# Plain float32 matmuls in place of three float32r products in a two-layer hybrid decoder (mLSTM, differential attention, routed experts)

## The chip, the cores and the metric

The kernel runs on one core of a Trainium2 chip. The metric is device time in microseconds (us) of one execution, the median over runs; lower is better. Engines are named as in the profile: PE is TensorE (matmuls), PEld its weight loads, DVE is VectorE, ACT is ScalarE, POOL is GpSimd, SP issues most of the DMAs.

## The reference

Two layers over 512 tokens of 1024 channels, all in float32. Each layer is a token mixer and then a mixture of experts; both read a normed input that is scaled and shifted by a modulation vector and both add their result, times a gate from the same vector, to the residual. Cut to what matters:

```python
D_MODEL, SEQ, DEPTH = 1024, 512, 2
A_HEADS, A_QK_DIM, A_V_DIM, A_CHUNK = 4, 128, 256, 128     # layer 0: mLSTM
B_HEADS, B_HEAD_DIM, B_V_DIM = 8, 64, 128                  # layer 1: differential attention
N_EXPERTS, N_GROUPS, TOP_K, D_EXPERT = 16, 4, 2, 512

def trunk(x, c, ...):
    for l in range(DEPTH):
        mod = silu(c) @ w_ada[l] + b_ada[l]                # 1024 x 6144: shift, scale, gate, twice
        sh1, sc1, g1, sh2, sc2, g2 = split(mod, 6)
        h = rms(x, norm1[l]) * (1 + sc1) + sh1
        x = x + g1 * (mlstm_mixer(h) if l % 2 == 0 else diff_attention(h))
        h = rms(x, norm2[l]) * (1 + sc2) + sh2
        x = x + g2 * grouped_moe(h, w_router, router_bias, w_gu[l], w_down[l])

def mlstm_mixer(h):
    proj = h @ w_in                                        # 1024 x 3080: q, k, v, o and 8 gate columns
    hout = mlstm_chunkwise(q, k, v, i_pre, log_f)          # 4 chunks of 128 tokens, a state between them
    return (rms(hout, h_norm) * sigmoid(o)) @ w_out        # 1024 x 1024

def diff_attention(h):
    q, k, v = split(h @ w_in)                              # 1024 x 3072
    a = softmax(q1 k1) - lam * softmax(q2 k2)              # per head, causal, q and k normed and rotated
    return rms(a @ v) @ w_out                              # 1024 x 1024

def grouped_moe(h):
    scores = sigmoid(h @ w_router)                         # one of 4 groups, the best 2 of its 4 experts
    for each expert e, tokens xb of e:
        gu = xb @ w_gu[e]                                  # 1024 x 1024
        yb = (silu(gu[:, :512]) * gu[:, 512:]) @ w_down[e] # 512 x 1024
    return sum over a token's two experts of gate_w * yb
```

## The kernel before

**Products.** Every large matrix product takes its weights from memory in float32 and makes two float32r parts of them: `split` (L205 to L210) copies the raw tile to `hi` on ACT (L208) and subtracts on DVE (L209; on POOL for the first strips) to get `lo`. The tokens are kept in two parts in the same way (`in_parts`, L343 and L344; `half_to_T`, L369 and L370). A product of 128 rows by 512 columns is then three matmuls that add up in one PSUM bank, high by high, high by low, low by high (`triple`, L212 to L217, for the experts and the output projections; L394 to L396 and L419 to L421 for the input projections):

```python
for ps, n, i in sorted(order, key=lambda o: o[1]) if last else order:
    w = (hi, lo, hi)[i][:, n * 512:(n + 1) * 512]
    T.matmul(ps, (xh, xh, xl)[i], w, start=first and i == 0, stop=last and i == 2)
```

In the names of the trace a trailing h or l is such a part: `guse64h` is the high part of row block 4 of expert 6's gate and up weights, `dnse50l` the low part of a block of expert 5's down weights. Transposes, attention scores, attention values, the mLSTM core and the routing are plain float32 matmuls already; so is the product of `diag` with the rows `yk` that come back from memory (L1278).

**Count of products.** The mLSTM's input projection has 192 products of 512 columns (q and k in `proj_cols`, v and o in `proj_rows`), the attention's 384 of 256 columns (12 strips `b00` to `bv6`), each output projection 64 of 512 columns (`out_proj`). An expert has 24 of 512 columns: 8 blocks of the inner dimension times `pg` and `pu`, then 4 blocks times `py0` and `py1`, on 128 gathered tokens; and 12 transposes of 128 columns (8 of its tokens, 4 of its activation). There are 16 experts in each layer.

**Order of the work.** The program is written out in order, with a small queue (`later`, `step`) that puts the latency-bound steps of the mixers (gates, chunks, heads, norms) between the steps of the projections; the framework's scheduler then orders the instructions of each engine, and each engine takes them in that order. One expert's pieces are put between those of the next: the transposes of the next tokens, the second half of gate and up, the first quarters of the next expert's, then the down product.

**Modulation.** `ada` (L225) loads four quarters of a 1024 x 1024 part of `w_ada`, scales each row block by an entry of silu(c) and adds them to `acc`: for layer 0 every other block in one step on DVE (L237), the rest as a scaling on ACT (L239) and an addition on POOL (L240). Six parts lie beside the mLSTM, four beside the attention.

**Weights ahead.** `load` issues the DMAs on SP into 4 buffers `raw` of 1 MB; for the experts `Prefetch` has 15 such places in all: 7 of its own, the 4 `raw` and the 4 in which the token parts lay.

**Results.** `keep` copies an expert's result from PSUM on ACT (L1332), multiplies it by the gate row on POOL (L1333) and scatters it to memory; the last expert's is added by matmuls (`results`, `add_to_tokens`), again in two parts.

Of the kernel before, what the change touches and what calls it, by code (L numbers as in the profile page):

```python
# [12 lines left out]
F32R = mybir.dt.float32r  # L13
# [8 lines left out]
P = 128  # L22
# [20 lines left out]
N_RAW = 4  # L43
N_RAW2 = 7
N_LO = 2
# [9 lines left out]
def trunk(ctx, tc, x, c, positions, norm1, norm2, w_ada, b_ada, a_w_in, a_b_if, a_h_norm, a_w_out,  # L55
# [7 lines left out]
    wsp = ctx.enter_context(tc.tile_pool(name="wsp", bufs=3))  # L63
# [15 lines left out]
    # Work of the tensor engine that waits for other engines is put between matmuls that don't.  # L79
# [35 lines left out]
    start = wsp.tile([P, 4, P], F32, tag="whi", name="start")  # L115
# [11 lines left out]
    def past(dst):  # L127
        """Column less row."""
# [43 lines left out]
    def hold(dst, kt=NK - 1):  # L172
        """Keeps a load from going ahead of those that the first matmuls wait for."""
# [31 lines left out]
    def split(raw, a, n, name, on=V):  # L205
        hi = wsp.tile([P, a, n], F32R, tag="whi", name=name + "h")
        lo = wsp.tile([P, a, n], F32R, tag="wlo", name=name + "l", bufs=N_LO)
        A.activation(hi, raw, AF.Copy)  # L208
        on.tensor_tensor(lo, raw, hi.bitcast(F32), op=ALU.subtract)  # L209
        return hi, lo  # L210

    def triple(p0, p1, xh, xl, hi, lo, first, last):  # L212
        hi, lo = hi.rearrange("p o n -> p (o n)"), lo.rearrange("p o n -> p (o n)")
        order = [(ps, n, i) for i in range(3) for n, ps in enumerate((p0, p1))]
        for ps, n, i in sorted(order, key=lambda o: o[1]) if last else order:
            w = (hi, lo, hi)[i][:, n * 512:(n + 1) * 512]
            T.matmul(ps, (xh, xh, xl)[i], w, start=first and i == 0, stop=last and i == 2)  # L217
# [7 lines left out]
    def ada(l, j):  # L225
        """Yields after each quarter of w_ada[l]'s columns of part j; their sums follow the last."""
# [1220 lines left out]
```

## Time and profile before

| | |
|---|---|
| median of 3 runs | 1370.02 us (1362.04, 1370.02, 1370.56) |
| profiled execution, first to last instruction | 1357.3 us |
| median less that span | 12.7 us |
| PE / PEld / DVE / ACT / POOL busy | 1210.1 / 956.6 / 1126.2 / 890.3 / 496.9 us |
| mean granted PE clock | 0.955 of full |

The profile gives the profiled execution's span; what lies around it is taken as the 12.7 us between it and the median. Matmuls overlap in the pipeline and a matmul's duration in the trace is longer than the time to the next one's start, so the rate of PE is read from the distance between starts. A plain float32 matmul leaves two records, a transpose or a float32r matmul one. The stages of the span are: start (0 to 34 us), the rest of layer 0's mixer with output projection and routing (to 316), its 16 experts (to 637), results and layer 1's projections with most heads (to 884), the last heads and the output projection (to 994), routing (to 1018), 16 experts (to 1338), the last results.

### The profile page before, as it was taken

How to read it: one execution, taken by the hardware profiler on the slowest of the kernel's cores; microseconds unless marked ns; L12 is line 12 of the kernel's file. 1: busy time of each engine (PE TensorE's matmuls, PEld its weight loads, DVE VectorE, ACT ScalarE, POOL GpSimd, SP SyncE). 2: the span in 40 equal slices, each digit the busy share in tenths (PEclk: the TensorE clock that was granted, in tenths of full speed). 3: DMA queues.
4: the chain of work that ended last, by engine and by line, in shares of the span. 5: the costliest groups of instructions: out<-in, count | busy, mean ns of one | idle time of the engine just before them, and what ended most of it. 6: DMA issues, size and time to landing. Idle time of an engine off the chain costs nothing. (4 is left out here: it accounts for less than half of the span.)

```text
span 1357.3 us, 18042 instructions
## 1 busy us (share of the span) xinstructions
PE 1210.1 (89%) x6082; PEld 956.6 (70%) x6082; DVE 1126.2 (83%) x1804; ACT 890.3 (66%) x1376; POOL 496.9 (37%) x305
## 2 busy tenths in 40 slices
PE   3899999887999999998899998878969999999996
PEld 3677777666777777775798878655747777777774
DVE  7956777877999999997867888867678999999996
ACT  5465666336777778775767676555537777877773
POOL 2644650821332332221552664524332233233211
PEclk7999999898999999999899999778979999999999
DMA  9777660757899999935351443304558999999904
GB/s 367 234 264 262 231 217 1 303 194 266 327 354 353 333 336 356 336 124 201 114 186 63 156 144 136 125 1 155 213 177 308 337 336 353 351 349 339 348 18 189
DMA packets 105586, 320.88 MB, mean 236 GB/s; under 512 B 14088, under 2 KB 26512, under 8 KB 104464
## 3 DMA queue, kind: packets, MB, share of 16 engines
q1 hardware_dynamic: 95120, 298.67, 60.3%
q0 software_dynamic: 10368, 20.99, 4.1%
q8 instruction: 50, 0.82, 0.2%
q14 instruction: 48, 0.39, 0.1%
HBM read 313.33 MB, written 23.07 MB: 248 GB/s over the span
## 5 line engine op out<-in xcount | busy, mean ns | idle before, releaser
L240 POOL TENSOR_TENSOR acc<-acc,ada 128x1024 f32<-128x1024 f32 x58 | 153.7, 2650 | 85.9 <-ACT ada L239 38.7
L1333 POOL TENSOR_TENSOR yoe<-yoe,grow 128x1024 f32<-128x1024 f32 x30 | 88.1, 2935 | 209.2 <-ACT yoe L1332 209.2
L1159 POOL DMA_INDIRECT xg<-h2d,lst x32 | 34.2, 1068 | 248.8 <-PE xTe L367 225.6
L239 ACT ACTIVATE ada<-ada,cact 128x1024 f32<-128x1024 f32 x58 | 64.7, 1144 | 31.4 <-DMA ada<-in_w_ada_dram 28.6
L864 ACT ACTIVATE p<-p,mx 128x128 f32<-128x128 f32 (+3 forms) x64 | 35.6, 557 | 38.2 <-DVE mx L863 38.2
L857 PE MATMUL s<-kTb,qTb 64*128 64x128 f32 (+3 forms) x128 | 45.9, 534 | 11.1 <-DVE mx L860 10.4
L307 POOL TENSOR_TENSOR qrs<-qrs,nhalf 128x4 f32<-128x4 f32 x32 | 36.0, 1131 | 51.0 <-DVE qrs L306 49.6
L1223 POOL DMA_INDIRECT yd<-yoe,lst x30 | 50.9, 1697 | 8.4 <-POOL yoe L1333 8.4
L367 PE MATMUL xTe<-ident,xg 128*128 128x128 f32 x256 | 39.0, 282 | 15.7 <-DMA xg<-h2d,lst 15.7
L452 POOL TENSOR_TENSOR wo<-wo,grow 128x1024 f32<-128x1024 f32 x16 | 40.1, 2528 | 29.6 <-DVE wos102l L209 14.9
L1194 ACT ACTIVATE acte<-pge 128x512 f32<-128x512 f32 (+1 forms) x34 | 19.2, 571 | 47.2 <-PE pge L217 47.2
L367 PEld LDWEIGHTS xTe<-ident,xg 128*128 128x128 f32 x256 | 32.1, 146 | 20.3 <-DMA xg<-h2d,lst 15.9
L860 DVE CUSTOM_DVE_ANT_0 p<-s,maskW 128x128 f32<-128x128 f32 (+3 forms) x64 | 29.9, 484 | 13.0 <-PE s L857 6.5
L307 POOL TENSOR_TENSOR ors<-ors,nhalf 128x2 f32<-128x2 f32 (+1 forms) x12 | 12.0, 1000 | 58.5 <-DVE ors L306 25.3
L237 DVE SCALAR_TENSOR_TENSOR acc<-ada,cact,acc 128x1024 f32<-128x1024 f32 x12 | 15.4, 1282 | 18.9 <-POOL acc L240 15.7
L857 PEld LDWEIGHTS s<-kTb,qTb 64*128 64x128 f32 x128 | 16.4, 200 | 19.6 <-DVE mx L860 12.0
L831 DVE TENSOR_TENSOR qrow<-qrow,qrs 128x256 f32<-128x256 f32 x32 | 24.3, 760 | 6.0 <-POOL qrs L307 5.9
L889 PE MATMUL o<-vb,aTs 128*128 128x128 f32 x160 | 26.7, 302 | 1.7 <-ACT aTs L881 0.9
L889 PEld LDWEIGHTS o<-vb,aTs 128*128 128x128 f32 x160 | 23.0, 210 | 6.7 <-ACT aTs L881 2.3
L369 ACT ACTIVATE xh0e<-xTe 128x512 fp32r<-128x512 f32 x32 | 19.0, 594 | 11.7 <-PE pue L217 7.1
L370 DVE TENSOR_TENSOR xl0e<-xTe,xh0e 128x512 fp32r<-128x512 f32 x32 | 21.9, 684 | 5.4 <-ACT xh0e L369 5.4
L251 PE MATMUL psada<-ident,acc 128*128 128x128 f32 x96 | 14.8, 287 | 13.0 <-DVE acc L276 12.4
(3698 smaller groups left out, 4866.1 us busy)
## 6 DMA issues: line engine op xcount, KB each, us to landing
we<-in_moe_w_gu_dram SPq DMA_DIRECT2D x128, 1024.0 KB, 6.8
we<-in_moe_w_down_dram SPq DMA_DIRECT2D x64, 1024.0 KB, 7.0
ada<-in_w_ada_dram SPq DMA_DIRECT2D x48, 1024.0 KB, 5.3
yk<-yd SPq DMA_DIRECT2D x8, 1024.0 KB, 6.9
wo<-in_a_w_out_dram SPq DMA_DIRECT2D x4, 1024.0 KB, 4.8
wo<-in_b_w_out_dram SPq DMA_DIRECT2D x4, 1024.0 KB, 4.7
x<-in_x_dram SPq DMA_DIRECT2D x4, 512.0 KB, 4.7
qk0w<-in_a_w_in_dram SPq DMA_DIRECT2D x2, 1024.0 KB, 13.7
```

Of the source, the lines that this page charges most:

```text
L239: A.activation(raw[:, k], raw[:, k], AF.Copy, scale=cact[:, kt:kt + 1])
L240: G.tensor_tensor(acc, acc, raw[:, k], op=ALU.add)
L307: G.tensor_tensor(r, r, nhalf[:, 0:ncol], op=ALU.pow)
L367: T.transpose(ps[:, k * P:(k + 1) * P], row[:, kt * P:(kt + 1) * P], ident)
L452: G.tensor_tensor(raw[:, k], raw[:, k], grow, op=ALU.mult)
L857: T.matmul(ps[:, 0:n], part(qTs, h)[q0:q0 + BHD, j * P:(j + 1) * P], part(kTs, h)[q0:q0 + BHD, 0:n], start=True, stop=True)
L860: V.tensor_tensor_reduce(p[:, 0:n], ps[:, 0:n], maskW[:, S - n:S], scale=1.0, scalar=NEG, op0=ALU.add, op1=ALU.max, accum_out=mx[:, cc:cc ...
L864: A.activation(p[:, 0:n], p[:, 0:n], AF.Exp, scale=0.125, bias=mx[:, cc:cc + 1], accum_out=mx[:, 2 + cc:3 + cc])
L889: T.matmul(po[:, 0:P], aT[:, kb * P:(kb + 1) * P], part(vs, h)[:, kb * P:(kb + 1) * P], start=kb == 0, stop=kb == j)
L1159: G.indirect_dma_start(out=xg, out_offset=None, in_=h2d[:, :], in_offset=bass.IndirectOffsetOnAxis(ap=itok, axis=0), bounds_check=S - 1, o ...
L1223: si = G.indirect_dma_start(out=yd[:, :], out_offset=bass.IndirectOffsetOnAxis(ap=irow, axis=0), in_=yo, in_offset=None, bounds_check=2 * ...
L1333: G.tensor_tensor(yo, yo, grow, op=ALU.mult)
```

## The change

The float32r parts go: no `split`, no `triple`, no `in_parts`. Each product is one float32 matmul on the loaded weights (`both`, and one `T.matmul` in each of the projections). Token operands are single float32 tiles. The gates and the router's logits are computed with tokens as the stationary operand, which saves a transposition afterwards. The modulation sums are all in one step on DVE but for the first row block. `keep` is one multiplication on DVE from PSUM. With the space of the parts free there are 8 `raw` buffers, and `Prefetch` has 17 places. The second half of the output projection multiplies its result by the gate on DVE, where the weights were multiplied on POOL before.

```diff
-N_RAW = 4
+N_RAW = 8
@@ load
-    def split(raw, a, n, name, on=V):
-        hi = wsp.tile([P, a, n], F32R, tag="whi", name=name + "h")
-        lo = wsp.tile([P, a, n], F32R, tag="wlo", name=name + "l", bufs=N_LO)
-        A.activation(hi, raw, AF.Copy)
-        on.tensor_tensor(lo, raw, hi.bitcast(F32), op=ALU.subtract)
-        return hi, lo
-    def triple(p0, p1, xh, xl, hi, lo, first, last):
...
+    def both(p0, p1, x, w, first, last):
+        for n, ps in enumerate((p0, p1)):
+            T.matmul(ps, x, w[:, n * 512:(n + 1) * 512], start=first, stop=last)
@@ ada
-                elif k == 0 and l == 0:
+                else:
                     V.scalar_tensor_tensor(acc, raw[:, k], cact[:, kt:kt + 1], acc, op0=ALU.mult, op1=ALU.add)
-                else:
-                    A.activation(raw[:, k], raw[:, k], AF.Copy, scale=cact[:, kt:kt + 1])
-                    G.tensor_tensor(acc, acc, raw[:, k], op=ALU.add)
@@ modulated
-            V.tensor_scalar(x, x, a1[k], sh, op0=ALU.mult, op1=ALU.add)
-            in_parts(*channels(h, hf * 4 + k), x)
+            V.tensor_scalar(channels(h, hf * 4 + k), x, a1[k], sh, op0=ALU.mult, op1=ALU.add)
@@ half_to_T
-        A.activation(dhi, pv3, AF.Copy)
-        V.tensor_tensor(dlo, pv3, dhi.bitcast(F32), op=ALU.subtract)
+        if hf:
+            A.activation(dst, pv3, AF.Copy)
+        else:
+            V.tensor_copy(dst, pv3)
@@ proj_rows (proj_cols likewise)
-                T.matmul(ps[t], xh, hi[:, k], start=kt == 0, stop=False)
-                T.matmul(ps[t], xh, lo[:, k], start=False, stop=False)
-                T.matmul(ps[t], xl, hi[:, k], start=False, stop=kt == NK - 1)
+                T.matmul(ps[t], at(t, kt), wt[:, k], start=kt == 0, stop=kt == NK - 1)
@@ out_proj
-                parts[kt] = split(raw[:, k:k + 1], 1, D, f"wos{l}{half}{kt}")
-                if half == 0:
-                    G.tensor_tensor(raw[:, k], raw[:, k], grow, op=ALU.mult)
+                parts[kt] = raw[:, k]
@@ gates_logits
-                    T.matmul(psg[0:16], wg[:, kt], xh, start=kt == 0, stop=False)
-                    T.matmul(psg[0:16], wg[:, kt], xl, start=False, stop=kt == NK - 1)
+                    for kt in range(NK):
+                        T.matmul(ps[:, t * 8:t * 8 + 8], at(t, kt), wg_raw[:, kt], start=kt == 0, stop=kt == NK - 1)
@@ gate_up, project_down
-                    hi, lo = split(raw(k), 1, D, f"gus{nm}{kt}")
-                    triple(pg, pu, *xs[kt], hi, lo, kt == 0, kt == NK - 1)
+                    both(pg, pu, xs[kt], raw(k), kt == 0, kt == NK - 1)
-                    hi, lo = split(raw(k), 1, D, f"dns{nm}{kt}")
-                    triple(py[0], py[1], ahi[:, kt], alo[:, kt], hi, lo, kt == 0, kt == 3)
+                    both(py[0], py[1], aT[:, kt], raw(k), kt == 0, kt == 3)
@@ act_T
-                in_parts(ahi[:, ks], alo[:, ks], pv3[:, ks])
+                A.activation(aT[:, ks], pv3[:, ks], AF.Copy)
@@ keep
-                A.activation(yo[:, n * 512:(n + 1) * 512], py[n], AF.Copy)
-            G.tensor_tensor(yo, yo, grow, op=ALU.mult)
+                cols = slice(n * 512, (n + 1) * 512)
+                V.tensor_tensor(yo[:, cols], py[n], grow[:, cols], op=ALU.mult)
```

On PE, in layer 0's experts, the down product of expert 5 for the first two of its four inner blocks is this before (other experts' rows stand between the second and the third):

```order
L217 MATMUL py0e_4093<-dnse50l,ahie_4062 128x512
L217 MATMUL py1e_4094<-dnse50l,ahie_4062 128x512
L217 MATMUL py0e_4093<-dnse50h,aloe_4063 128x512
L217 MATMUL py1e_4094<-dnse50h,aloe_4063 128x512
L217 MATMUL py0e_4093<-dnse51h,ahie_4062 128x512
L217 MATMUL py1e_4094<-dnse51h,ahie_4062 128x512
L217 MATMUL py0e_4093<-dnse51l,ahie_4062 128x512
L217 MATMUL py1e_4094<-dnse51l,ahie_4062 128x512
L217 MATMUL py0e_4093<-dnse51h,aloe_4063 128x512
L217 MATMUL py1e_4094<-dnse51h,aloe_4063 128x512
```

And this is the whole down product of expert 5 in the changed kernel:

```order
L204 MATMUL py0e_2612<-we_2401,aTse_2599 128x512
L204 MATMUL py1e_2613<-we_2401,aTse_2599 128x512
L204 MATMUL py0e_2612<-we_2401,aTse_2599 128x512
L204 MATMUL py1e_2613<-we_2401,aTse_2599 128x512
L204 MATMUL py0e_2612<-we_2419,aTse_2599 128x512
L204 MATMUL py1e_2613<-we_2419,aTse_2599 128x512
L204 MATMUL py0e_2612<-we_2419,aTse_2599 128x512
L204 MATMUL py1e_2613<-we_2419,aTse_2599 128x512
```

The matmuls now read the loaded tiles `we` themselves and stand together; 24 rows have become 8.

On DVE, in layer 1's attention, the low part of a weight strip (`b12s4l`) stood between the steps of the heads (L860 is the masked maximum of the scores `s`, L869 and L870 the softmax rows `p`, `mx` their maxima and sums, L828 the sums of squares `qss` of q and k):

```order
L869 TENSOR_SCALAR p011_6659<-p011_6659,mx01_6650 128x128
L837 TENSOR_TENSOR qrow_6635<-qrow_6635,rot_6645 128x4x16
L870 TENSOR_TENSOR p010_6653<-p010_6653,p011_6659 128x128
L209 TENSOR_TENSOR b12s4l_6875<-b12w0_6814,b12s4h_6874 128x1024
L828 TENSOR_REDUCE qss_6681<-qsq_6680 128x4
L860 ISA p100_6736,mx10_6733<-s100_6734,maskW_5899 128x256
```

In the changed kernel the steps of the modulation sum `acc13` stand between the same steps of the heads (now L817, L820):

```order
L224 SCALAR_TENSOR_TENSOR acc13_4219<-ada130_4220,cact_101,acc13_4219 128x1024
L817 ISA p021_4313,mx02_4304<-s021_4311,maskW_3371 128x128
L817 ISA mx02_4304 128x1
L224 SCALAR_TENSOR_TENSOR acc13_4219<-ada131_4282,cact_101,acc13_4219 128x1024
L820 TENSOR_SCALAR mx02_4304<-mx02_4304 128x1
L224 SCALAR_TENSOR_TENSOR acc13_4219<-ada131_4282,cact_101,acc13_4219 128x1024
```

The subtractions for the weight strips are gone from DVE's row, and the sums that POOL and ACT shared have come into it, seven for each part.

## Rows read from the trace of the kernel before

**Rows 1.** The page's head and part 1: span, busy time of each engine.

```profile
span 1357.3 us, 18042 instructions
PE 1210.1 (89%) x6082; PEld 956.6 (70%) x6082; DVE 1126.2 (83%) x1804; ACT 890.3 (66%) x1376; POOL 496.9 (37%) x305
```

**Rows 2.** Busy time by stage: window, length, engines, clock, DMA share, GB/s.

```profile
0.00:34.00 34.00, 12.43 (x50) 10.64 (x51) 24.07 (x55) 18.80 (x33) 9.45 (x22) 0.76 0.96 367
34.00:316.00 282.00, 252.57 (x1212) 199.21 (x1211) 209.07 (x398) 151.90 (x233) 139.55 (x84) 0.95 0.60 211
316.00:637.00 321.00, 301.40 (x1352) 235.04 (x1350) 293.91 (x272) 242.68 (x286) 88.03 (x46) 0.99 0.81 301
637.00:884.00 247.00, 226.33 (x1547) 192.11 (x1548) 200.85 (x549) 162.78 (x385) 123.84 (x74) 0.94 0.40 139
884.00:994.00 110.00, 94.17 (x452) 69.94 (x450) 74.16 (x175) 57.37 (x136) 35.31 (x23) 0.88 0.34 129
994.00:1018.00 24.00, 11.14 (x88) 8.90 (x88) 17.47 (x76) 10.31 (x17) 10.28 (x10) 0.71 0.51 179
1018.00:1338.00 320.00, 300.77 (x1357) 234.97 (x1355) 294.12 (x271) 243.18 (x286) 88.08 (x46) 1.00 0.81 300
1338.00:1357.30 19.30, 11.26 (x33) 5.81 (x32) 12.59 (x15) 3.23 (x4) 2.36 (x1) 0.96 0.43 174
```

**Rows 3.** Timeline of PE, float32r matmuls of 512 columns, an expert: start, duration.

```profile
1140.18 0.40 PE L217 MATMUL py1e<-dnse50l,ahie 128*128 128x512 f32 x1
...
1142.98 0.39 PE L217 MATMUL py1e<-dnse52l,ahie 128*128 128x512 f32 x1
```

**Rows 4.** Timeline of PE, float32r matmuls of 256 columns, an attention strip.

```profile
702.74 0.28 PE L396 MATMUL b02p<-b02s0h,bl 128*128 128x256 f32 x1
...
704.02 0.28 PE L395 MATMUL b02p<-b02s0l,bh 128*128 128x256 f32 x1
```

**Rows 5.** Timeline: plain float32, 512 columns, eight records in a row.

```profile
646.36 3.60 PE L1278 MATMUL pce<-yk,diag 128*128 128x512 f32 x8
```

**Rows 6.** Line L1278, durations in ns (least, median, most) of loads and matmuls.

```profile
L1278 PEld LDWEIGHTS pce<-yk,diag x32: 187/190/192, 640.6 to 1350.3; 128*128 128x128 f32 x32
L1278 PE MATMUL pce<-yk,diag x32: 590/592/595, 640.9 to 1350.7; 128*128 128x512 f32 x32
```

**Rows 7.** Groups of PE by form: plain float32 of 257 columns (busy, mean ns).

```profile
L646 PE MATMUL n<-core,qi 128*128 128x257 f32 x24 | 7.2, 380 | 0.0
```

**Rows 8.** Chain that ended last, layer 1's experts: start, us, step.

```profile
1128.62 3.17 DVE guse57l L209
1131.83 0.73 PE pge L217 x2
...
1148.32 3.16 DVE guse67l L209
1151.52 0.73 PE pge L217 x2
...
1277.48 0.87 PE xTe L367 x8
```

**Rows 9.** Timeline of expert 6's end: start, duration, what ended PE's wait.

```profile
1147.43 2.96 POOL L1333 TENSOR_TENSOR yoe<-yoe,grow 128x1024 f32<-128x1024 f32 x1 [5.99 <-ACT yoe L1332]
...
1151.52 0.50 PE L217 MATMUL pge<-guse67l,xh1e 128*128 128x512 f32 x1 [1.17 <-DVE guse67l L209]
```

**Rows 10.** The page's part 5, the modulation sums: busy, mean ns.

```profile
L240 POOL TENSOR_TENSOR acc<-acc,ada 128x1024 f32<-128x1024 f32 x58 | 153.7, 2650 | 85.9 <-ACT ada L239 38.7
...
L239 ACT ACTIVATE ada<-ada,cact 128x1024 f32<-128x1024 f32 x58 | 64.7, 1144 | 31.4 <-DMA ada<-in_w_ada_dram 28.6
...
L237 DVE SCALAR_TENSOR_TENSOR acc<-ada,cact,acc 128x1024 f32<-128x1024 f32 x12 | 15.4, 1282 | 18.9 <-POOL acc L240 15.7
```

**Rows 11.** Busy time of line L209 (low parts) on DVE and POOL, by stage.

```profile
637.00:884.00 247.00, 31.64 (x23) 4.67 (x2) 0.94 0.40 139
```

**Rows 12.** Waits of PE from 975 to 1018 us: total, times, longest.

```profile
PE xTe L367 <- DMA xg<-h2d,lst: 7.9, 1, 7.9
PE psp L1062 <- DVE ohb L1051: 3.0, 1, 3.0
```

More of the change, by code (lines that the diff above doesn't have):

```diff
@@ L12 @@
 F32 = mybir.dt.float32
-F32R = mybir.dt.float32r
 BF16 = mybir.dt.bfloat16
@@ L112, in give @@
         live[what] -= 1
-    start = wsp.tile([P, 4, P], F32, tag="whi", name="start")
+    start = const.tile([P, 4, P], F32, name="start")
     crow, vrow, vrow2, jp = start[0:NK, 0], start[:, 1], start[0:16, 2], start[:, 3]
@@ L326, in operand @@
     def operand(pool, shape, name):
-        return [[pool.tile(shape, F32R, tag=f"h{c}{i}", name=f"{name}{c}{i}") for i in range(2)] for c in "hl"]
+        return [pool.tile(shape, F32, tag=f"h{i}", name=f"{name}{i}") for i in range(2)]
     def channels(h, kt):
-        return [p[kt // 4][:, kt % 4] for p in h]
+        return h[kt // 4][:, kt % 4]
     def tokens(h, t):
-        return [p[t // 2][:, t % 2] for p in h]
+        return h[t // 2][:, t % 2]
     def scale_of(l, k4):
@@ L382, in strip @@
             for k in (0, a):
-                yield k0 + k, split(raw[:, k:k + a], a, n, f"{name}s{k0 + k}", G if name in ("qk0", "b00") else V)
+                yield k0 + k, raw[:, k:k + a]
                 next(mix, None)
@@ L433, in products @@
                 run_first()
-            triple(ps[t, 0], ps[t, 1], *(p[:, kt] for p in tokens(h, t)), *parts[kt], kt == 0, kt == NK - 1)
+            both(ps[t, 0], ps[t, 1], tokens(h, t)[:, kt], parts[kt], kt == 0, kt == NK - 1)
             if kt == NK - 1:
@@ L791, in attention @@
         h = operand(outer, [P, 2, NK, P], "b")
-        at = lambda t, kt: [p[:, kt] for p in tokens(h, t)]
+        at = lambda t, kt: tokens(h, t)[:, kt]
         with ExitStack() as st:
@@ L910, in heads_turn @@
             def heads_turn(j, h0, nh):
-                take("aT", 2)
-                give("aT")
                 n = nh * P
@@ L1146, in __init__, with slot @@
             self.parts, self.n, self.ready = sequence(l), 0, []
-            self.outer = [(outer, f"h{c}{i}", 1) for i in range(2) for c in "hl"]
-            self.slots = [(early if i < N_EARLY[l] else ahead, f"raw2{i}", 1) for i in range(N_RAW2)] + self.outer[:2] + [None] * N_RAW + self.outer[2:]
+            held = [(outer, f"h{i}", 1) for i in range(2)]
+            self.slots = [(early if i < N_EARLY[l] else ahead, f"raw2{i}", 1) for i in range(N_RAW2)] + held[:1] + [None] * N_RAW + held[1:]
+        def slot(self):
+            self.n += 1
+            return self.slots[(self.n - 1) % len(self.slots)]
         def more(self, n=1, after=None):
             for part in islice(self.parts, n):
-                self.ready.append(load(part, 2, D, f"we{self.n}", self.slots[self.n % len(self.slots)], after))
-                self.n += 1
+                self.ready.append(load(part, 2, D, f"we{self.n}", self.slot(), after))
     def moe(l, pool, grow, fetch, xgs, lst, count, past, pk, eid):
@@ L1166, in turn @@
         def turn(state, xg, hf, nm):
-            xhi, xlo = (pool.tile([P, 4, P], F32R, tag=f"x{c}{hf}", name=f"x{c}{hf}{nm}") for c in "hl")
-            half_to_T(xg, hf, xhi, xlo, f"xT{nm}{hf}")
-            state[0].extend((xhi[:, k], xlo[:, k]) for k in range(4))
+            xT = pool.tile([P, 4, P], F32, tag=f"x{hf}", name=f"x{hf}{nm}", bufs=2)
+            half_to_T(xg, hf, xT, f"xT{nm}{hf}")
+            state[0].extend(xT[:, k] for k in range(4))
         def weights(ch):
```

122 lines of the change are left out of this document (40 added, 82 removed).

## The prediction

> **What bounds the kernel now.** I read the busy times first, then the stages, then the distance between matmul starts, and last the chain that ended last. PE is busy for 1210 of 1357 us, DVE for 1126 [rows 1]; by stage PE has 301 of 321 us in layer 0's experts and 301 of 320 in layer 1's, 253 of 282 in layer 0's mixer, 226 of 247 in most of layer 1's [rows 2]. Busy time counts the pipeline's tail, so the load on PE is better taken from its starts. In an expert, 13 float32r matmuls of 512 columns start within 2.80 us, 0.233 us apart [rows 3], so the three that make a product take 0.70 us. In the attention, 12 starts of 256 columns lie within 1.28 us, 0.116 apart [rows 4], and a product takes 0.35.
>
> An expert has 24 products and 12 transposes; eight transposes take 0.87 us, 0.109 each [rows 8]. That is 24 x 0.70 + 12 x 0.109 = 18.1 us of PE. The period of an expert, between the same split of experts 5 and 6, is 19.70 us [rows 8]. The missing 1.6 us are seen in the chain: a low part takes 3.15 us on DVE while POOL multiplies a result (2.96 us), and PE waits 1.17 us for it [rows 8, 9]. So in the experts PE is the bound, and the splits on DVE cost it 8%. In the mixers PE is nearest to the bound too, but the chains of heads and gates leave gaps, and the granted clock falls to 0.94 and 0.88 of full, that is, part of the time was at 1.2 instead of 2.4 GHz [rows 2].
>
> **The change, part by part.** *The price of a float32 product* decides. It is in the trace: eight records of plain float32 with 512 columns, each with its own weights, take 3.60 us [rows 5]; less the last one's 0.592 [rows 6], that is 3.01 us over seven distances, 0.430 each. A product leaves two records: 0.86 us against 0.70, or 0.16 more. For 256 columns the nearest row is 257 columns: a record lasts 0.380 against 0.592 us for 512 [rows 6, 7], 0.212 less, so 0.218 from start to start, and a product takes 0.43 against 0.35, or 0.08 more.
>
> The Trainium skill, page FP8 and Floating Point Precision, section TensorE Precision Notes, states that true float32 makes four passes through the array. Against three parts of one pass each that would be 4/3 of 0.70, 0.93 us; rows 3 and 5 give 1.23 times, since a float32r matmul takes longer here than a quarter of the float32 product. That case is among the rivals below.
>
> *Experts.* 24 x 0.86 + 1.3 = 21.9 us each, 351 us for 16. What hid behind PE or held it up goes: the split on ACT and DVE, and POOL's multiplication. The loads cover it: DMA has 0.81 of its share at 320 us a stage [rows 2], so some 260 us would do, and two more places ahead cost and give nothing. In the new order some experts' first tokens are transposed directly ahead of their use, which lets PE wait for one copy; I add 2 us a stage. 353 against 321 and 320: **+32 and +33**. Bounds: +29 with no such wait, +46 with a wait of 1 us for each.
>
> *Layer 0's mixer (34 to 316 us).* 192 products x 0.16 = 31, the output projection's 64 x 0.16 = 10, the gates 64 records of 0.109 for 16 matmuls of 0.233, 3: together +44. PE idles for 29 us there [rows 2]. Of these, 13 stay: they belong to routing and to the gather of the first tokens, as in the like stage of layer 1, where PE has 11 of 24 us and waits 7.9 and 3.0 [rows 2, 12]. The other 16 are waits for splits, for the modulation and for the mLSTM's chain; with longer matmuls between and less on DVE and ACT I take 15 as filled: **+29**. Bounds: +44, nothing filled; +20, all filled and the first product 8 us earlier, since its token parts and the low part on POOL are gone.
>
> *Layer 1 to 884 us.* 384 x 0.08 = 31, the last expert's result 8 x 0.86 for 16 x 0.233, 3: +34. PE idles 21 us, and at a clock of 0.94 loses some 13 more [rows 2]. DVE was busy for 201 of 247 us. It loses 32 us of low parts [rows 11] and gains 28 steps of 1.28 us, 36 [rows 10], so it keeps its load in a longer stage; POOL's 28 additions of 2.65 us and ACT's scalings of 1.14 [rows 10] vanish. I take 22 us of these gaps as filled: **+12**. Bounds: +34 and 0.
>
> *884 to 994 us.* 64 x 0.16 = +10; PE idles for 16 of 110 us and loses 11 by the clock of 0.88 [rows 2], much of it beside splits of the output weights; I take 18 as filled: **-8**. Bounds: +10 and -16.
>
> *The rest.* Routing loses one copy and one transposition per tile and gains nothing else: **0**. The last result gains 3 us of matmuls and loses 2 of parts: **+1**. The start is limited by loads (DMA 0.96 of its share [rows 2]): 0.
>
> Sum: 29 + 32 + 12 - 8 + 33 + 1 = **+99 us**. On the span of 1357.3 that is 1456; with the 12.7 us that lie between span and median, **1469 us**, 7% over 1370.
>
> **Rivals.**
>
> 1. *Faster: weight loads set PE's pace, not columns.* If each matmul record cost what a load and its start cost, 0.233 us, two records would replace three and a product would take 0.47. An expert then needs 12.5 us of PE, the loads become the bound at some 260 us a stage [rows 2], 60 less each, and the mixers gain perhaps 25: about 1225. It decides from the point where a product takes less than (19.70 - 1.3) / 24 = 0.77 us. For it: PEld is busy for 70% of the span [rows 1]. Against it: a load takes 0.190 us and its float32 matmuls still start 0.430 apart [rows 5, 6]. The Trainium skill, page Perfetto Trace Analysis, section Identifying the Most-Contended Engine, calls matmul busy time a bad measure for TensorE and names the busy share of weight loads as one of two better ones; by that measure the fewer loads would be a gain, and rows 5 and 6 speak against it.
>
> 2. *No change.* A product at 0.77 us, or gaps that give back all of the 99 us. The experts have only 1.6 us of gap in 19.70 to give for 3.8 more of matmuls, so this needs another price: 1370.
>
> 3. *A product at 4/3 of the three parts, 0.93 us*: 0.07 more on 1088 products of 512 columns and 0.035 on 384 of 256, 90 us on top, 1558. Against it: rows 5 and 6.
>
> 4. *The sums on DVE hold up the heads.* Each step waits for its load at the head of DVE's row, and behind it wait the masked maxima and softmax rows of the heads, for which ACT and then PE wait. If that eats the filled gaps of layer 1 (22 + 18 us), 1509. For it: DVE's share of 81% there [rows 2]. Against it: loads have six tenths of their share free, and the additions were waited for before as well.
>
> 5. *The new order costs 1 us per expert* (tokens copied just in time): 14 us more a stage, 1497.
>
> 6. *The mixers fill all they can* (+20, 0, -16): 1440.
>
> **How the numbers follow.** Forecast 62%, rivals 1 to 6: 2, 2, 2, 10, 12 and 10%. Predicted is the forecast's 1469. The range reaches to rival 6 below, 1438, and above to 1505, where rival 5 and most of rival 4 lie; some 20% is left out. A change of less than 1% can hardly be told from none here (the three runs differ by 0.6%). Faster by over 1%: rival 1 and what is cheaper than rival 2, 0.02; within 1%: 0.02; slower: 0.96.
>
> **What would show it.** In the changed profile: float32 records of 512 columns 0.43 us apart, and an expert's period near 22 us instead of 19.70; PE without waits for DVE in the experts; DVE and ACT far below half there; the DMA share at some 0.74 in the experts; layer 1's stages to 994 us together not much longer than before, with a clock nearer to full. The prediction is wrong if a product takes 0.77 us or less, if the period is over 23 us (waits of PE for copies or loads), or if layer 1's mixer gets 30 us longer, with PE waiting behind DVE.

## The result, and the profile after

The changed kernel takes **1462.8 us** (median of 4 runs, 1462.1 to 1464.5) where the kernel before took 1366.0 (1360.3 to 1370.6) beside it: 1.070 times, 95% interval 1.066 to 1.075. Forecast were 1469 us and a slower kernel. The profiled execution spans 1459.5 us, 102 more than before; forecast were 99 more.

The page's head and part 1 of the changed kernel, as [rows 1]:

```profile
span 1459.5 us, 13078 instructions
PE 1384.5 (95%) x4662; PEld 770.3 (53%) x4662; DVE 488.2 (33%) x1369; ACT 300.0 (21%) x715; POOL 164.0 (11%) x193
```

DVE has lost 638 us of work, ACT 590 and POOL 333, over a quarter of all instructions is gone, and the kernel is slower: PE alone got 174 us more.

Busy time by stage, with the stages cut where the same work begins and ends as in [rows 2]:

```profile
34.00:352.00 318.00, 296.75 (x1001) 164.69 (x999) 150.15 (x378) 70.62 (x142) 27.19 (x41) 0.93 0.53 193
352.00:709.00 357.00, 354.55 (x969) 167.00 (x968) 45.50 (x77) 30.89 (x53) 31.20 (x31) 0.99 0.76 260
709.00:951.00 242.00, 240.62 (x1142) 187.61 (x1142) 151.93 (x525) 102.36 (x306) 45.07 (x43) 1.00 0.42 149
951.00:1050.00 99.00, 93.02 (x389) 52.14 (x388) 42.73 (x149) 38.67 (x119) 15.94 (x18) 1.00 0.44 167
1050.00:1084.00 34.00, 17.94 (x114) 16.95 (x113) 18.27 (x96) 9.28 (x15) 6.89 (x8) 0.59 0.35 125
1084.00:1442.00 358.00, 355.55 (x976) 167.63 (x975) 46.92 (x79) 31.71 (x53) 32.27 (x32) 1.00 0.75 261
```

In the experts PE works almost without a gap (355 of 357 us), DVE has 13% and the loads 0.76 of their share. In layer 1's mixer the idle time of PE is gone (1.4 us of 242, before 20.7 of 247) and the clock is full. After the start, most of PE's idle time lies in the two routings: 16 of the 34 us from 1050 to 1084, where the granted clock is 0.59 of full, so that most of them are at the lower level of 1.2 GHz, and 12 of 30 in layer 0's. Some 9 us are left in layer 0's mixer and 6 in the last heads and projection.

To compare stages without a window's edges I took, in both traces, the start of the same matmuls as marks:

| stage, between the same matmuls | before | after | change | forecast |
|---|---|---|---|---|
| start to the first product | 32.6 | 29.8 | -2.8 | 0 |
| layer 0's mixer, to the last output projection | 257.8 | 292.5 | +34.7 | +29 with routing |
| layer 0's routing, to the first expert | 25.1 | 29.8 | +4.7 | (in the 29) |
| layer 0's experts | 322.0 | 357.0 | +35.0 | +32 |
| layer 1, to the last product of the strips | 246.3 | 241.7 | -4.6 | +12 |
| to the last output projection | 110.5 | 99.2 | -11.3 | -8 |
| layer 1's routing | 24.6 | 34.8 | +10.2 | 0 |
| layer 1's experts | 320.4 | 355.9 | +35.5 | +33 |
| last results | 11.5 | 13.4 | +1.9 | +1 |

A routing ends in this table with the first expert's first product, and the last results with the start of their last matmul. There is one trace of each kernel. That of the kernel before is one of its shorter executions: it spans 1357.3 us, and the executions of the same kernel beside the experiments span 1357.4 to 1368.7. A difference of a few us in a single stage is therefore no more than executions of one kernel can differ by.

### The profile page after: what moved, and what is told of

It is laid out like the page before. It is cut to its first block, busy times and chain, and to the rows that moved or that the text cites. A ratio compares the mean times of both kernels' runs of the same rounds, so it can differ in the third digit from the quotient of the medians.

```text
span 1459.5 us, 13078 instructions
## 1 busy us (share of the span) xinstructions
PE 1384.5 (95%) x4662; PEld 770.3 (53%) x4662; DVE 488.2 (33%) x1369; ACT 300.0 (21%) x715; POOL 164.0 (11%) x193
## 5 line engine op out<-in xcount | busy, mean ns | idle before, releaser
L204 PE MATMUL pge<-we,x0e 128*128 128x512 f32 x256 | 133.7, 604 | 2.7 <-DVE x0e L350 2.7
L204 PE MATMUL pue<-we,x0e 128*128 128x512 f32 x256 | 131.6, 596 | 0.0
L204 PE MATMUL py0e<-we,aTse 128*128 128x512 f32 x256 | 131.1, 593 | 0.0
L204 PE MATMUL pge<-we,x1e 128*128 128x512 f32 x256 | 131.0, 593 | 0.0
L204 PE MATMUL py1e<-we,aTse 128*128 128x512 f32 x256 | 130.7, 592 | 0.0
L204 PE MATMUL pue<-we,x1e 128*128 128x512 f32 x256 | 130.7, 592 | 0.0
L224 DVE SCALAR_TENSOR_TENSOR acc<-ada,cact,acc 128x1024 f32<-128x1024 f32 x70 | 89.7, 1282 | 2.0 <-DMA ada<-in_w_ada_dram 0.8
L204 PEld LDWEIGHTS pue<-we,x0e 128*128 128x128 f32 x256 | 49.1, 192 | 62.5 <-issue 62.5
L204 PE MATMUL po<-wo,h 128*128 128x512 f32 x128 | 59.9, 616 | 0.0
L204 PE MATMUL po<-wo,o 128*128 128x512 f32 x128 | 57.3, 594 | 0.2 <-ACT o L872 0.2
```

The source lines that it names most:

```text
L204: T.matmul(ps, x, w[:, n * 512:(n + 1) * 512], start=first, stop=last)
```

## The experiments

Each is compared with the kernel before, run in turn with it on the same chip; ratios are to that, with 95% intervals.

### The experts' products alone

```diff
 # kernel before, in gate_up; project_down, turn, act_T and keep as in the change
-                    hi, lo = split(raw(k), 1, D, f"gus{nm}{kt}")
-                    triple(pg, pu, *xs[kt], hi, lo, kt == 0, kt == NK - 1)
+                    both(pg, pu, xs[kt], raw(k), kt == 0, kt == NK - 1)
...
```

> The kernel before, with only the experts' products as plain float32 matmuls and their results multiplied on DVE from PSUM; both mixers, the modulation sums and the 4 raw buffers as before. Theory (PE's columns set the price: 24 products of 0.86 us and 12 transposes, 21.9 us an expert): the two expert stages become 357 us each, as in the changed kernel, the rest stays, so 1366 + 36 + 37 = about 1439 us, and the period of an expert is 21.9 us. Rival (the buffers, the order or the sums made the experts longer, not the products): under 1400 us.

Measured: 1436.5 us, ratio 1.051 (1.047 to 1.055). The expert stages take 357.4 and 356.4 us, and their period is that of the changed kernel, 21.9 us on average (it alternates between 18.5 and 25.4, as the order puts more of the next expert ahead in every second one). By window, PE and the loads have the numbers of the changed kernel:

```profile
316.00:674.00 358.00, 354.13 (x972) 166.90 (x971) 46.85 (x80) 32.56 (x55) 31.98 (x32) 1.00 0.77 268
1061.00:1417.00 356.00, 353.21 (x969) 166.51 (x968) 45.81 (x78) 31.92 (x54) 31.32 (x32) 1.00 0.77 267
```

So some 72 of the 97 us come from the experts alone (their products, and their results multiplied on DVE), with neither the buffers nor the sums nor the mixers changed.

### The buffers alone

```diff
 # changed kernel
-N_RAW = 8
+N_RAW = 4
```

> The changed kernel with 4 raw weight buffers in place of 8, so 13 places ahead instead of 17 for the experts. Theory (PE is the bound, loads have a quarter of their share free): no change within 5 us of 1463. Rival (the distance of the loads matters, in the experts or in the mixers): over 1475 us, with waits of PE for loads.

Measured: 1463.9 us, against 1462.8; ratio to the kernel before 1.074 (1.071 to 1.078). The expert stages are 355.5 and 357.0. Four buffers more are worth nothing where PE is the bound.

### What bounds the experts before: no low parts, then one part

```diff
 # kernel before, in split: no low part of a weight, the high part stands in for it
...
-        on.tensor_tensor(lo, raw, hi.bitcast(F32), op=ALU.subtract)
-        return hi, lo
+        return hi, hi
```

> The kernel before without the subtraction that makes a weight's low part: the high part is used in its place, so that each product keeps its three float32r matmuls and the result is not the reference's. Theory (PE's 0.70 us per product is the bound of the experts, the splits on DVE cost them 8%): expert stages of about 300 us for 320, layer 1's mixer some 12 us shorter, about 1310 us. Rival (DVE is the bound and PE only looks busy): with DVE relieved the expert stages fall towards what the loads need, 260 to 280 us, and the kernel to 1240 to 1280 us.

```diff
 # and in triple, proj_rows, proj_cols: the high by high matmul alone
-        order = [(ps, n, i) for i in range(3) for n, ps in enumerate((p0, p1))]
+        order = [(ps, n, 0) for n, ps in enumerate((p0, p1))]
...
```

> The kernel before with a single float32r matmul for each product, high part by high part, and no low parts of weights; the result is not the reference's. It lowers the price of a product to 0.233 us. Theory (by the prediction's first rival the loads then set the pace): expert stages of 260 to 265 us at a DMA share near 1, the mixers bound by loads and by the chains of heads, about 1150 us. Rival (something other than PE and loads holds the experts, such as the copies on ACT or the gathers): expert stages of 290 us or more.

Measured: 1284.5 us (0.942, 0.936 to 0.949) without low parts of weights, and 1124.2 us (0.825, 0.819 to 0.831) with one part. Neither computes what the kernel before computes. The window of layer 0's experts, first of the kernel without low parts, then of that with one part:

```profile
306.00:602.00 296.00, 291.76 (x1352) 237.63 (x1351) 47.55 (x82) 242.96 (x289) 68.01 (x47) 1.00 0.87 323
```

```profile
261.00:512.00 251.00, 177.15 (x588) 101.01 (x586) 48.94 (x82) 232.24 (x289) 66.97 (x46) 0.85 0.97 381
```

With DVE all but idle (48 us of 296) the stage falls only to 296 us, and the period to 18.0 us in most experts: that is the 18.1 us of PE that the prediction counted (24 x 0.70 + 1.3). PE was the bound of the experts before, and the splits on DVE cost 1.7 us of 19.7. Layer 0's mixer and layer 1's, with their 251 and 240 us, gave 7 and 6 us, and the last projection 7. The kernel as a whole came out 26 us under the 1310 expected, near the rival's 1280; what speaks against the rival is the length of the stages, 296 us and not 260 to 280. With one part PE is idle for 74 of 251 us and the DMA share is 0.97: now the loads are the bound, at 251 us a stage, where the prediction's first rival had some 260 and the expectation 260 to 265. ACT, still copying the high parts, is busy for 232 of them; it is not shown that the loads would need all of the 251 without it.

Put in a row, the price of a product and the period of an expert are 0.233 and 15.4 us on average (loads), 0.70 and 18.0 (PE), 0.70 and 19.7 (PE and a wait for DVE), 0.86 and 21.9 (PE).

### POOL's multiplication of the results

```diff
 # kernel before, in keep
-                A.activation(yo[:, n * 512:(n + 1) * 512], py[n], AF.Copy)
-            G.tensor_tensor(yo, yo, grow, op=ALU.mult)
+                cols = slice(n * 512, (n + 1) * 512)
+                V.tensor_tensor(yo[:, cols], py[n], grow[:, cols], op=ALU.mult)
```

> The kernel before, with one part of the change alone: an expert's result is multiplied by the gate row on DVE straight from PSUM, where ACT copied it and POOL multiplied it. All products stay in three float32r parts. Theory (POOL's multiplication holds up one low part per expert on DVE, 3.15 us, for which PE waits 1.17 us): that wait goes, DVE takes 1.3 us per expert for the results and gets back about 2, the expert stages shorten by some 17 us each, about 1332 us. Rival (DVE, busy for 294 of 321 us there, becomes the bound with more work): no gain, 1366 to 1385 us.

Measured: 1352.0 us, ratio 0.992 (0.990 to 0.995). The expert stages shorten by 11 us each (311.2 and 309.5), not by 17; the period is 18.8 us. The group of the same low part on DVE as in [rows 8], of this kernel (busy us, mean ns):

```profile
L209 DVE TENSOR_TENSOR guse67l<-we,guse67h 128x1024 fp32r<-128x1024 f32 x1 | 1.2, 1219 | 0.0
```

It took 3.14 us beside POOL's multiplication [rows 8, 9] and takes 1.22 without it. The rows show how: the multiplication ended at 1150.39 us (1147.43 and 2.96), the low part at 1151.48 (1148.32 and 3.16), 1.1 us later, which is about its own length. So it waited for the multiplication to end and was not merely slowed. Of the 1.7 us that PE lost in an expert this change gives 0.9 back (19.7 to 18.8). But 12 us are lost again in layer 1's mixer and projection (256.9 and 112.3 us; in the mixer the granted clock is 0.91, before 0.94), in which no line was changed; the first experiment has 6 us of the same. With layer 1 in plain float32 it is 3 us (the mixes below). What it comes from is not settled; part of it can be the difference between executions.

### Layer 1's mixer: plain matmuls, then the sums

```diff
 # kernel before, layer 1 only: strips (proj_rows) and out_proj read the loaded weights; no
 # parts of tokens; second half of out_proj: results times the gate on DVE, not weights on POOL
+                if lo is None:
+                    T.matmul(ps[t], xh, hi[:, k], start=kt == 0, stop=kt == NK - 1)
+                    continue
...
```

> The kernel before, with only layer 1's mixer (strips and output projection) in plain float32 matmuls; its modulation sums stay on ACT and POOL. Theory (the gaps of PE there came from DVE's low parts, and longer matmuls fill them): the two stages to the last output projection shorten by the 16 us seen in the changed kernel, about 1350 us. Rival (the gaps came from the modulation sums on POOL and ACT, which the change moved to DVE): the 44 us of added matmul time are only partly filled and the kernel gets slower, 1370 to 1395 us.

```diff
 # and, in ada, layer 1's own four sums
-                elif k == 0 and l == 0:
+                elif l and j > 1 or k == 0 and l == 0:
                     V.scalar_tensor_tensor(acc, raw[:, k], cact[:, kt:kt + 1], acc, op0=ALU.mult, op1=ALU.add)
```

> As the run before, and layer 1's own four modulation sums in one step each on DVE. Theory: no further change, 1350 us within 5, since DVE has lost as much as it gains. Rival (the sums on POOL made the gaps): 1350 us here, but 20 to 40 us less than with the sums on ACT and POOL. Prediction's rival 4 (the sums hold up the heads on DVE): 10 to 40 us more than with the sums on ACT and POOL.

```diff
 # changed kernel, in ada: the sums as before
+                elif k == 0 and l == 0:
+                    V.scalar_tensor_tensor(acc, raw[:, k], cact[:, kt:kt + 1], acc, op0=ALU.mult, op1=ALU.add)
                 else:
-                    V.scalar_tensor_tensor(acc, raw[:, k], cact[:, kt:kt + 1], acc, op0=ALU.mult, op1=ALU.add)
+                    A.activation(raw[:, k], raw[:, k], AF.Copy, scale=cact[:, kt:kt + 1])
+                    G.tensor_tensor(acc, acc, raw[:, k], op=ALU.add)
```

> The changed kernel with the modulation sums as before (half or all of the row blocks scaled on ACT and added on POOL). Theory: no change within 5 us of 1463, since PE has hardly a gap in the mixers. Rival (the sums on DVE filled layer 1's gaps): 1475 to 1500 us, layer 1's mixer longer. Prediction's rival 4 (they hold up the heads): under 1455 us.

Measured: 1357.1 us with plain matmuls alone, ratio 0.994 (0.991 to 0.997); 1345.6 with the sums on DVE as well, 0.985 (0.982 to 0.989); and the changed kernel with the sums back on ACT and POOL 1470.8, 8 us more than the changed kernel. From the first pce to the last output projection the mixer takes 356.8 us before, 351.7 plain, 338.6 plain with the sums on DVE. Neither my theory (all 16 us from the matmuls) nor its rival (all from the sums) holds: the plain matmuls, by the count 41 us longer on PE (384 x 0.08 and 64 x 0.16), are worth 5, and the sums 13 (by the medians of the kernels 8 and 11). In the changed kernel, too, the sums matter for layer 1's mixer: to the last product of the strips it takes 241.7 us with them on DVE and 254.1 with them on POOL, and to the last output projection 340.9 and 350.6.

Why should 28 more steps on DVE make the mixer shorter? The groups of DVE's steps in that stage (busy us, mean ns of one), first with the sums on POOL:

```profile
L840 DVE TENSOR_TENSOR qrow<-qrow,qrs 128x256 f32<-128x256 f32 x31 | 23.0, 743 | 10.2 <-POOL qrs L307 10.2
L878 DVE TENSOR_SCALAR p<-p,mx 128x128 f32<-128x128 f32 (+3 forms) x22 | 14.7, 670 | 0.6
L837 DVE TENSOR_REDUCE qss<-qsq 128x4 f32<-128x256 f32 x31 | 12.6, 413 | 16.4 <-ACT qsq L836 16.4
L877 DVE SCALAR_TENSOR_TENSOR mx<-mx,nlam 128x1 f32<-128x1 f32 x22 | 11.1, 505 | 0.6
L1282 DVE TENSOR_TENSOR x<-x,pce 128x512 f32<-128x512 f32 x8 | 5.0, 676 | 0.0
```

Then with the sums on DVE:

```profile
L837 DVE TENSOR_REDUCE qss<-qsq 128x4 f32<-128x256 f32 x31 | 12.7, 416 | 10.0 <-ACT qsq L836 9.9
L840 DVE TENSOR_TENSOR qrow<-qrow,qrs 128x256 f32<-128x256 f32 x30 | 12.7, 423 | 13.0 <-POOL qrs L307 12.9
L878 DVE TENSOR_SCALAR p<-p,mx 128x128 f32<-128x128 f32 (+3 forms) x21 | 7.8, 374 | 0.5
L1282 DVE TENSOR_TENSOR x<-x,pce 128x512 f32<-128x512 f32 x8 | 5.0, 676 | 0.0
L877 DVE SCALAR_TENSOR_TENSOR mx<-mx,nlam 128x1 f32<-128x1 f32 x21 | 4.6, 219 | 0.5
```

The mean of the multiplication of q and k by their norm (L840, two operands from SBUF) falls from 743 to 423 ns, that of the scaling of the probabilities (L878, four lengths of row in one mean) from 670 to 374, that of the small step on the maxima (L877) from 505 to 219; the reduction with one operand (L837) and the addition that reads PSUM (L1282) don't change. With 28 steps of 1.28 us more, DVE is busy for 154 us in place of 170.

The means mislead about how this happens. The same line with its least, median and most (ns), first with the sums on POOL, then with them on DVE:

```profile
L840 DVE TENSOR_TENSOR qrow<-qrow,qrs x32: 408/425/2582, 665.2 to 898.5; 128x256 f32<-128x256 f32 x32
```

```profile
L840 DVE TENSOR_TENSOR qrow<-qrow,qrs x32: 412/424/427, 663.2 to 887.6; 128x256 f32<-128x256 f32 x32
```

The medians are equal. Of the 32 steps 27 take 0.41 to 0.43 us beside the additions as well, and five take 2.1 to 2.6. One of the five, with the reduction before it and POOL's addition (start, us):

```profile
871.20 2.40 POOL L240 TENSOR_TENSOR acc<-acc,ada 128x1024 f32<-128x1024 f32 x1
871.30 0.41 DVE L837 TENSOR_REDUCE qss<-qsq 128x4 f32<-128x256 f32 x1
871.63 2.25 DVE L840 TENSOR_TENSOR qrow<-qrow,qrs 128x256 f32<-128x256 f32 x1
```

The addition ends at 873.60, the multiplication 0.28 us later; the reduction runs through beside the addition. So most steps lose nothing, and a few wait until an addition that is running has ended. L877 is alike: 28 of its 32 steps take 0.21 to 0.22 us, four 0.86 to 2.17.

### POOL busy as long, but reading nothing

```diff
 # layer 1's mixer plain, sums on ACT and POOL; the sums of layer 1's modulation are left out
-                    G.tensor_tensor(acc, acc, raw[:, k], op=ALU.add)
+                    if l and j > 1:
+                        for n in (D, D, D // 2):
+                            G.memset(raw[:, k, 0:n], 0.0)
+                    else:
+                        G.tensor_tensor(acc, acc, raw[:, k], op=ALU.add)
```

> Layer 1's mixer plain with its sums on ACT and POOL, as in the second run, but POOL's 28 additions of 2.4 us are replaced by writes of zeros into the loaded block, together about 2.45 us, which read nothing; the modulation of layer 1 is left out by it. Theory (a POOL step that reads SBUF makes those DVE steps wait that read two operands or scalars from SBUF): the multiplication of q and k by their norm goes back from 0.74 to about 0.42 us and the mixer from 249 to about 241 us, 1346 to 1350 us in all. Rival (POOL's row is long, and the powers of the norms wait behind the additions in it): the multiplication's duration may change, but the mixer stays at 247 us or more and the kernel at 1355 us or more.

Measured: 1348.6 us, ratio 0.990 (0.986 to 0.994). POOL is busy for as long as with the additions (109 us in this stage in both). The same groups of this kernel (four lines further down in its code):

```profile
L844 DVE TENSOR_TENSOR qrow<-qrow,qrs 128x256 f32<-128x256 f32 x31 | 13.1, 423 | 14.4 <-POOL qrs L311 14.3
L882 DVE TENSOR_SCALAR p<-p,mx 128x128 f32<-128x128 f32 (+3 forms) x23 | 11.0, 479 | 0.6
L841 DVE TENSOR_REDUCE qss<-qsq 128x4 f32<-128x256 f32 x31 | 12.6, 416 | 27.4 <-ACT qsq L840 27.3
L881 DVE SCALAR_TENSOR_TENSOR mx<-mx,nlam 128x1 f32<-128x1 f32 x23 | 5.1, 220 | 0.6
```

The multiplication is at 423 ns again, and its longest step takes 0.44 us:

```profile
L844 DVE TENSOR_TENSOR qrow<-qrow,qrs x32: 411/424/440, 662.8 to 889.3; 128x256 f32<-128x256 f32 x32
```

DVE is busy for 135 us in the stage where it was busy for 170 beside the additions (first with the additions, then with the writes):

```profile
639.00:888.00 249.00, 242.93 (x1148) 189.44 (x1149) 170.43 (x508) 132.35 (x341) 109.28 (x72) 0.99 0.39 133
637.00:886.00 249.00, 243.01 (x1160) 190.22 (x1160) 134.61 (x520) 136.54 (x351) 108.58 (x128) 0.99 0.39 135
```

So the additions cost DVE 36 us there by their reading of SBUF, not by their length in POOL's row. The Trainium skill, page SBUF — State Buffer, section Who interferes with whom, says that a VectorE instruction with two SBUF inputs contends with a GpSimd instruction that reads SBUF, not with one that only writes it. The trace agrees for L840: five of its 32 steps wait beside the additions and none beside the writes. Steps on a single tensor do wait for the writes at times: the scaling of the probabilities (L878, L882) has a longest step of 2.48 us beside the additions, 1.20 beside the writes and 0.49 without either, and the step ahead of the power of the norms (128x4) 2.30, 0.96 and 0.17.

What this is worth to the kernel is less clear. To the last output projection 9 of the 13 us are back (342.3 against 351.7 and 338.6), but not where they were expected: to the strips' last product it takes 249.4 us as before, where some 241 were expected, and the gain shows behind it, 92.9 us to the end of the projection for 102.3, with the granted clock at full where it was 0.93. In the strips 3.6 us are one wait of PE ahead of the modulation's own matmuls, which the other run does not have there. The run also takes the chain of additions away, on which the modulation waits, and the scheduler orders the rows of PE somewhat differently. That the 9 us come from DVE's waits is therefore likely, and not shown alone.

### The router's logits

```diff
 # changed kernel: logits as before, weights stationary, then a transposition
...
-                T.matmul(ps, xT[:, kt], awr[:, kt], start=kt == 0, stop=kt == NK - 1)
+                T.matmul(ps[0:NE, 0:P], awr[:, kt], xT[:, kt], start=kt == 0, stop=kt == NK - 1)
+            lT = pool.tile([NE, P], F32, tag="lT", name=f"lT{t}", bufs=2)
+            A.activation(lT, ps[0:NE, 0:P], AF.Copy)
+            later(1, lambda: logits_T(t, lT, h2))
...
```

> The changed kernel with the router's logits as before: the weights stationary, 16 rows by 128 columns, and a transposition after them. Theory (routing got longer because the logits fall behind the output projection in PE's order, whatever their form): routing of layer 1 stays near 35 us and that of layer 0 near 30, 1463 us. Rival (the new form itself, 16 columns for each load of 128 x 128 tokens, makes it longer): routing back to 25 to 30 us, about 1453 us.

Measured: 1454.6 us, 8 us less than the changed kernel; ratio 1.068 (1.064 to 1.071). Of these 8 us, 4.5 are in layer 1's routing (30.3 us for 34.8), and 2 each in layer 0's routing (28.0 for 29.8) and its mixer. My theory is refuted in its number; the rival's number came (about 1453, routing of 25 to 30 us). The timeline of PE in layer 1's routing (start, us, what ended the idle time), first of the changed kernel:

```profile
1050.79 4.84 PE L965 MATMUL psr<-awr,x2T 128*128 128x16 f32 x40
1061.16 0.17 PE L1007 MATMUL psp<-ohb,before 128*128 128x16 bf16 x1 [5.53 <-DVE ohb L996]
...
1063.08 1.90 PE L1023 MATMUL psl<-told,hot 128*128 128x32 f32 x8
1064.78 3.57 PE L965 MATMUL psr<-awr,x2T 128*128 128x16 f32 x16
...
1072.22 0.17 PE L1007 MATMUL psp<-ohb,before 128*128 128x16 bf16 x1 [2.07 <-DVE ohb L996]
```

Then with the logits as before:

```profile
1053.88 1.92 PE L965 MATMUL psr<-x2T,awr 128*16 128x128 f32 x16
...
1060.54 0.17 PE L1013 MATMUL psp<-ohb,before 128*128 128x16 bf16 x1 [2.66 <-DVE ohb L1002]
...
1063.39 0.20 PE L1013 MATMUL psp<-ohb,before 128*128 128x16 bf16 x1
```

With the new form the last tile's logits (16 records at 1064.78) stand behind the placement of the first two tiles (psp, psl) in PE's row, and that placement waits 5.5 us for DVE's choice: so the two choices, which run side by side on DVE in the other form, come one after the other. By these rows it is the place in the row that costs, more than PE's time for the form: 40 records take 4.84 us, 0.12 each, and in the old form 16 take 1.92, 0.12 each; only the 16 late ones take 3.57, 0.22 each, in the stretch at the lower clock. No run moved the place with the form kept. The other 5 us of routing (30 against 24.6) are in every run with a plain projection and the old logits; before, the first tiles' choices lay beside the second half of the projection, which is shorter and denser now. That this is their cause is argued from the order of the rows; no run had it alone.

### Putting together what paid

```diff
 # experts and layer 0's mixer in three parts as before; layer 1's mixer plain, with
 # its sums on DVE (third run); results multiplied on DVE (fifth run)
```

> Parts of the change put together that each paid or should: experts and layer 0's mixer in three float32r parts as before; layer 1's mixer in plain float32 with its modulation sums on DVE; results multiplied on DVE. Theory: the gains add up, 1346 - 34 = about 1312 us. Rival of the run before: 1346 us or more.

```diff
 # and layer 0's sums on DVE too
-                elif l and j > 1 or k == 0 and l == 0:
+                elif True:
```

> The mix of parts that was fastest so far (experts and layer 0's mixer in three parts, layer 1's mixer plain, results and layer 1's sums on DVE), and layer 0's modulation sums on DVE too. Theory (POOL's additions lengthen DVE's steps that read two operands from SBUF, in layer 0 as in layer 1): 5 to 10 us less than 1332. Rival (DVE, busy for 192 of 257 us in layer 0's mixer with its low parts, has no room for 30 steps of 1.28 us more): the same or up to 15 us more.

Measured: 1331.7 us, ratio 0.977 (0.974 to 0.981), and 1330.4 us, 0.976 (0.971 to 0.982). The first is 29 us under the kernel before beside it and 14 under the third run's 1345.6: in the traces the expert stages shorten by 10 and 12 us (310.4 and 310.2), and the stages between and the last results give 9 back. It misses the 1312 expected because the results on DVE were worth some 11 and not 17 us a stage. With layer 0's sums on DVE its mixer is 5 us shorter (255.7 us for 260.9) and its routing 3 us longer; the totals can't be told apart, so the 5 to 10 us expected are not seen. Both compute all that the kernel before computes, and both are faster than either kernel, by some 2% than the kernel before.

## Why the prediction was right, step by step

**The price of a product: right.** In the changed kernel the records of 512 columns stand 0.429 us apart (median), 0.430 forecast from [rows 5]; those of 256 stand 0.216 apart, 0.218 forecast. An expert, from the timeline of PE, with one pair of records for each product:

```profile
1189.76 1.04 PE L345 MATMUL xTe<-ident,xg 128*128 128x128 f32 x8
1191.31 1.13 PE L204 MATMUL pge<-we,x0e 128*128 128x512 f32 x2 [0.51 <-DVE x0e L350]
1192.27 1.02 PE L204 MATMUL pue<-we,x0e 128*128 128x512 f32 x2
1193.13 1.02 PE L204 MATMUL pge<-we,x0e 128*128 128x512 f32 x2
1193.98 1.02 PE L204 MATMUL pue<-we,x0e 128*128 128x512 f32 x2
```

Products start 0.86 us apart; the duration of 1.02 holds the pipeline's tail. Rival 3 (four thirds of the three parts) and rivals 1 and 2 (0.77 or less) are out. On rival 1: the busy share of weight loads, one of two measures that the Trainium skill (page Perfetto Trace Analysis, section Identifying the Most-Contended Engine) prefers to that of matmuls, fell from 70 to 53% while PE's idle time in layer 0's experts went from 20 us of 321 to 2 of 357; here that measure points the wrong way, and the distance of starts told it. The Trainium skill's four passes (page FP8 and Floating Point Precision, section TensorE Precision Notes) can't be told apart in any run here; a quarter of the 0.859 us is 0.215. The ratio is 1.23 and not 4/3 since a float32r matmul takes 0.233 us and not 0.215.

**Experts, +32 and +33: right in mechanism, 3 us short each.** The period is 21.92 us on average, 21.9 forecast. The stage before was 322.0, though 16 periods of 19.70 are 315: some 7 us of ends, which I left out of the 353; with them and the 2 us of waits the sum would be 360, and 357 were measured. The waits that I added for the new order (2 us a stage) are there, as PE's list of waits from 380 to 709 us shows (total, times, longest):

```profile
PE pge L204 <- DVE x0e L350: 1.3, 2, 0.8
PE aTe L1151 <- DVE acte L1142: 0.6, 1, 0.6
PE aTe L1151 <- ACT aTse L1152: 0.5, 1, 0.5
```

Rival 5, a microsecond for each expert, is out.

**Layer 0's mixer, +29: too low.** The first expert's products start 36.5 us later. From 34 us to the last output projection, before and after:

```profile
34.00:291.00 257.00, 240.59 (x1127) 189.86 (x1126) 191.54 (x322) 140.51 (x215) 130.61 (x73) 0.97 0.61 217
34.00:322.00 288.00, 279.06 (x910) 148.51 (x909) 133.11 (x304) 65.08 (x133) 20.42 (x33) 0.97 0.54 198
```

PE has 38 us more of work there, and some 3 more lie ahead of 34 us since the first product starts 2.8 us earlier: 41 of the gross 44. Of the 16 us of its idle time outside of routing only 7.5 were filled, not 15: 8.9 are left. The routing behind it, put at nothing, adds 5. Of what is left, 5.0 us are one wait, which ends at 55 us, for the second half of the first tokens (DVE `a`), and 1.9 a wait for the gates' weights.

**Layer 1, +12: too high, the wrong step of the prediction.** It priced the sums as load: 36 us more on DVE against 32 less, "so it keeps its load". In fact DVE's load fell from 201 to 152 us, since with the additions gone no step of DVE waits for them any more (the runs on the sums); that price was in [rows 8, 9], where a low part took 3.15 us beside POOL's multiplication, and I read it as the multiplication's cost and not as a cost of any POOL step that reads SBUF. PE's idle time went from 20.7 to 1.4 us and the clock from 0.94 to full, so that more than the 34 us gross came back. Rival 4 had the right place and the wrong sign: moved to DVE, the sums shorten the stage by 12 us in the changed kernel.

**884 to 994 us, -8: right** (-11.3), with the clock from 0.88 to full. **Routing, 0: wrong**, +10 in layer 1 and +5 in layer 0: I counted its instructions and not their places in PE's row, and not that the projection, once it is denser, no longer covers the first tiles. **Last result, +1, and the start, 0: right** within 3 us. **The median**: its distance from the profiled span was 12.7 us before and is 3.3 now, so that the median moved by 97 us and the span by 102. The 12.7 us that the prediction added do not lie around an execution: in every run whose own span is on record, the time is 1.7 to 2.6 us over it. They come, as far as the record shows, from setting the span of a short execution beside the median of three that lie up to 9 us apart. The terms' errors, +7, +3, -17, -3, +10 and +2.5, largely cancel; that the total is nearer than its parts is in part luck.

## What to carry to other kernels

Where PE is the bound, taking work off the other engines buys little (all low parts of weights gone, 1.7 of 19.7 us an expert), and the price of a matmul in its new form decides; read it from the distance of starts of the same form elsewhere in the trace, and check the bound with a run that leaves the suspected engine's work out (18.0 us against 18.1 counted). Plain float32 paid here only in layer 1's mixer, where other engines held PE up, and a mix of both forms beats the kernel before by 2%. Before moving work between DVE and POOL, compare the longest and the median duration of the same DVE step with POOL at work and at rest; a mean hides that a few steps wait for long.

## What the runs showed of the hardware that I had not expected

- A DVE step with two operands in SBUF (128x256) takes 0.42 us beside POOL's additions too, but five of 32 waited for an addition to end and took 2.1 to 2.6 us; with POOL as busy but only writing, the longest took 0.44. A step that reads PSUM keeps its mean of 676 ns, and the reduction with one operand its 413 to 416.
- A wait costs the same however small the step: four of 32 steps on one column (128x1) with a second operand in SBUF took 0.86 to 2.17 us in place of 0.22.
- Some DVE steps on a single tensor wait for POOL's writes as well: a step of 128x4 took up to 0.96 us beside them, and 0.17 at most without.
- A float32r matmul of 512 columns takes 0.233 us from start to start, a quarter of the plain product 0.215.
